# A two-layer hybrid encoder trunk: where the statistics of the MLP norm stand among the block products

## The chip, the cores and the metric

The kernel runs on one core of a Trainium2 chip. Its time is device microseconds of one execution; the figure quoted is the median of several. Times inside an execution come from one profiled execution, in microseconds from the start of its span. Engines: PE (TensorE), DVE (VectorE), ACT (ScalarE), POOL (GpSimd) and SP, which issues most of the DMAs.

## The reference, cut to what matters

```python
for i in range(DEPTH):                      # DEPTH = 2; D_MODEL = SEQ = 1024, D_FF = 4096
    h = rmsnorm(x, norm_mix_g[i])
    ...                                     # layer 0: RWKV-7 and DeltaNet heads; layer 1: chunked attention
    x = x + mix
    hf = rmsnorm(x, norm_ffn_g[i])
    x = x + jnp.square(jax.nn.relu(hf @ mlp_w1[i])) @ mlp_w2[i]
    x = x + rmsnorm(p[i] @ ple_w_proj[i], ple_norm_g[i]) * jax.nn.sigmoid(x @ ple_w_gate[i])

def rmsnorm(x, g, eps=NORM_EPS):
    xf = x.astype(jnp.float32)
    y = xf * lax.rsqrt(jnp.mean(xf * xf, -1, keepdims=True) + eps)
    return (y * g.astype(jnp.float32)).astype(x.dtype)
```

The norm in question is the one before the MLP. Its row factor is one number for each of the 1024 positions. Since relu(c z)^2 = c^2 relu(z)^2 for a positive c, the kernel multiplies by the square of that factor behind the first MLP product, not ahead of it, so the first products can run before the factor is known.

## The kernel before, in words

The program has a mixer stage and a function `tail` for each of the two layers. Activations are held transposed, features in the 128 partitions and the 1024 positions along the free dimension, in two halves of 512. Every float32 product is made of three matmuls of a high and a low part (`mm3`).

`tail` first finishes the output projection of the mixer and writes the new x to DRAM (`self.xh`, `self.xh2`, eight row blocks each). The MLP follows in a block scheme with seven products where eight are usual. The first MLP product is cut into 16 units `p`. In a unit there are seven block products (`product(p, m)`, 12 matmuls of 128x512 each, so 84 in a unit) in the order m = 1, 2, 5, 6, 7, 3, 4; slot (p, q) is the q-th of them. Their left operands are split weights, prepared one unit ahead by `prepare` (on ACT and DVE); their right operands `cmb[m]` stand in tiles that the profile calls `r` (m = 1, 2, 7, 3), `xw` and `x` (m = 5, 6) and `act` (m = 4). The results are combined on DVE (`plus`, L1375), then squared by `hidden` on ACT (L1380, L1381). The first four units (`PLAIN`) store the result without the row factor. From unit 4 on `hidden` multiplies by `rs` (L1385), so `rs` must be ready there.

`rs` is made in three steps:

- `squares(n)`, for n = 0 to 7: two DMAs on SP's queue bring the two halves of block n into one tile `xq` (L1315), ACT squares each half in place (L1317), and DVE adds it to one of two accumulators `acc` (L1318). There is one buffer for `xq`, so a DMA waits for the two adds of the block before.
- `row_stats`: eight matmuls against a column of ones (the profile's `dps<-ones,acc`, two instructions each, four matmuls for each accumulator), and on DVE eleven small operations of 128x8, of which the last nine are three Newton steps for the inverse root in `col` (L289, L290, L291).
- `to_rows`: eight transposes of `col` (`dps<-ident,col`), two copies by ACT into `rs` (L386), and one squaring on DVE (L1496).

The instructions are written out in program order, and a scheduler with a timeline of its own then sets the order in each engine's queue. Each queue is worked off in that order. The results of all products go to a ring of eight PSUM banks (`bank`), which the statistics use too.

Of the kernel before, what the change touches and what calls it, by code (L numbers as in the profile page):

```python
# [12 lines left out]
ALU = mybir.AluOpType  # L13
# [7 lines left out]
NK = D // P  # L21
# [88 lines left out]
class Trunk:  # L110
# [1092 lines left out]
    def tail(self, i, xsrc):  # L1203
# [10 lines left out]
        V, A, G = nc.vector, nc.scalar, nc.gpsimd  # L1214
        last = i == 1
        hs = [slice(0, HB), slice(HB, T)]
        with ExitStack() as es:
# [28 lines left out]
            def tiles_x(dt):  # L1246
                xw = [self.xp.tile([P, 3, T], dt, tag=f"xw{q}", name=f"xw{q}") for q in range(2)]
                return ([xw[k // 3][:, k % 3, :] for k in range(6)] +
                        [self.xp.tile([P, T], dt, tag=f"x{k}", name=f"x{k}") for k in (6, 7)])
# [11 lines left out]
            accs = [self.accp.tile([P, HB], F32, tag=f"acc{hf}", name="acc") for hf in range(2)]  # L1261
            col = self.cst.tile([P, NT], F32, tag="col", name="col")
# [4 lines left out]
            def split(c, s):  # L1267

                hi, lo = c[:, 0], c[:, 1]
                if len(s.shape) > 2:  # L1270
                    hi, lo = (z.rearrange("p (j c) -> p j c", c=P) for z in (hi, lo))
                A.copy(hi, s)  # L1272
                V.tensor_tensor(lo, s, hi.bitcast(F32), op=ALU.subtract)  # L1273
# [36 lines left out]
            def squares(n):  # L1310

                both = self.pre.tile([P, 2, HB], F32, tag="pl", name="xq")
                for hf, src in ((0, self.xh[n]), (1, self.xh2[n])):
                    t = both[:, hf]
                    nc.sync.dma_start(out=t, in_=src)  # L1315
                    if n:
                        A.activation(t, t, AF.Square)  # L1317
                        V.tensor_tensor(accs[hf], accs[hf], t, op=ALU.add)  # L1318
                    else:
                        A.activation(accs[hf], t, AF.Square)  # L1320
# [3 lines left out]
            def raws(p):  # L1324
                r = lt[3 - p % 2] if p else place(F32)
                for e in range(2):
                    nc.sync.dma_start(out=r[:, e], in_=a["w1"][i, 2 * p + e])
                prep[p] = [r[:, u].rearrange("p (j e c) -> p e j c", e=2, c=P)[:, v] for u in range(2) for v in range(2)], {}, []

            def prepare(p, m):  # L1330

                (a11, a12, a21, a22), d, free = prep[p]
                if (p, m) == (0, 1):
                    d[m] = self.pre.tile([P, 2, HB], F32R, tag="pl", name="w1")
                else:
                    if not free:
                        free += parts(place(F32R))
                    d[m] = free.pop(0)
                if m == 5:

                    V.tensor_tensor(a21, a21, a22, op=ALU.add)
                o, u, v = {1: (a11, None, None), 2: (a12, None, None), 5: (a21, None, None), 6: (a11, a21, a11),
                           4: (a22, None, None), 7: (a22, a22, a11), 3: (a12, a12, a11)}[m]
                if u is not None:
                    V.tensor_tensor(o, u, v, op=ALU.subtract)
                split(d[m], o)
# [16 lines left out]
            rs = self.pre.tile([P, T], F32, tag="ph", name="rs")  # L1363


            def product(p, m):
                ps, c = self.bank(), prep[p][1][m]
                for j in range(4):
                    o, z = slice(j * P, j * P + P), cmb[m][j]
                    self.mm3(ps, c[:, 0, o], c[:, 1, o], z[:, 0], z[:, 1], j == 0, j == 3)  # L1370
                return ps

            def plus(t, u, out=None):
                r = out if out is not None else scr()
                V.tensor_tensor(r, t, u, op=ALU.add)  # L1375
                return r

            def hidden(t, p, r, hf):

                A.activation(t, t, AF.Relu)  # L1380
                A.activation(t, t, AF.Square)  # L1381
                if p < PLAIN:
                    nc.scalar.dma_start(out=self.hd[2 * p + r][:, hs[hf]], in_=t)
                else:
                    V.tensor_tensor(t, t, rs[:, hs[hf]], op=ALU.mult)  # L1385
                    if (r, hf) != (0, 1):
                        store(p, {(0, 0): 1, (1, 0): 2, (1, 1): 3}[r, hf], t)
                return t
# [4 lines left out]
            def differ(p, m, u, v, out=None):  # L1393
                t = out if out is not None else scr()
                V.tensor_tensor(t, u, v, op=ALU.subtract)
                store(p, m, t)
                return t
# [4 lines left out]
            def load_w2(g, u):  # L1402
                t, raw = place(F32R), self.pre.tile([P, 2, HB], F32, tag="pl", name="w2")
                for j in range(2):
                    nc.sync.dma_start(out=raw[:, j], in_=a["w2"][i, 2 * g + j, u])
                split(t, raw.rearrange("p j c -> p (j c)"))
                w2[g, u] = t[:, 0], t[:, 1]

            def fetch_hidden(g, k, t, raw):
                nc.sync.dma_start(out=raw, in_=self.hd[4 * g + k])  # L1410
                return t, raw

            def load_hidden(t, raw):
                V.tensor_tensor(raw, raw, rs, op=ALU.mult)
                split(t, raw)
# [32 lines left out]
                split(areas[m][q % 4], raw)  # L1448

            prep_order = (1, 2, 5, 6, 4, 7, 3)  # L1450
            for m in prep_order[1:]:
                prepare(0, m)
            for p in range(16):
                if p < 15:
                    raws(p + 1)
                else:
                    load_w2(0, 0)
                for q, m in enumerate(order):
                    ps = product(p, m)
                    if m == 1:  # L1460
                        p1 = scr()
                        A.copy(p1, ps)
                    elif m == 2:
                        c11 = hidden(plus(p1, ps), p, 0, 0)
                    elif m == 5:
                        p5 = ps
                    elif m == 6:
                        u2 = plus(p1, ps, p1)
                        u4 = plus(u2, p5)
                    elif m == 7:  # L1470
                        u3 = plus(u2, ps, u2)
                        c22 = hidden(plus(u3, p5), p, 1, 1)
                    elif m == 3:
                        c12 = hidden(plus(u4, ps, u4), p, 0, 1)
                        if p >= PLAIN:
                            differ(p, 7, c22, c12)
                            t1 = differ(p, 5, c12, c11, c12)
                            t2 = differ(p, 6, c22, t1)
                    else:
                        c21 = hidden(plus(u3, ps, u3), p, 1, 0)  # L1480
                        if p >= PLAIN:
                            differ(p, 4, c21, t2)
                    if p < 15:
                        prepare(p + 1, prep_order[q])
                    elif q == 1:
                        hid = [fetch_hidden(0, k, h0[k], lt[2 + k // 2][:, k % 2]) for k in range(4)]
                    elif 2 <= q < 6:
                        load_hidden(*hid[q - 2])
                    yield 0
                if p < 3:  # L1490
                    for n in range(3 * p, min(3 * p + 3, NK)):
                        squares(n)
                if p == 2:
                    self.row_stats(accs, col)
                    self.to_rows(col, rs)
                    V.tensor_tensor(rs, rs, rs, op=ALU.mult)  # L1496
            x = tiles_x(F32)
            for k in range(NK):
                nc.sync.dma_start(out=x[k][:, hs[0]], in_=self.xh[k])
# [602 lines left out]
```

## Time and profile before

| | |
|---|---|
| median of 3 runs | 3133.64 us (3126.05 to 3135.7) |
| the profiled execution | 3130.04 us, its span 3128.3 us |
| mean granted TensorE clock | 0.968 |
| PE busy | 3000.5 us, 96% of the span |
| DVE busy | 2234.1 us, 71% |
| ACT busy | 1510.6 us, 48% |
| squares, first and last DMA, layer 0 | 999.88 and 1045.47 us |
| statistics on PE, layer 0 | 1050.03 to 1059.4 us |
| squares, first and last DMA, layer 1 | 2406.13 and 2451.93 us |
| statistics on PE, layer 1 | 2456.86 to 2463.4 us |

A busy PE is not a PE at its peak: the granted clock is 1.0 or 0.5, and matmuls overlap. In a timeline, each row has the start, the time until the last of the group has ended, the engine, the line, the operation with its tiles, the count and, in brackets, the idle time ahead of it and what ended that.

### The profile page before, as it was taken

What the parts mean: (1) busy time and instruction counts of PE and PEld (TensorE: products, weight loads), DVE (VectorE), ACT (ScalarE), POOL (GpSimd) and SP (SyncE); (2) the same over time, 40 slices, a digit from 0 to 9 for tenths busy, and PEclk for the clock granted to TensorE, in tenths of its full rate; (3) what the DMA queues carried; (4) which work ended last, traced back from release to release, by engine and by line L of the source; (5) the groups of instructions that cost most, each with busy time, mean ns of one, the idle gap of its engine ahead of it and who ended that gap; (6) DMA issues with size and microseconds to landing.
All of it is one profiled execution on the core that took longest, in us unless ns stands there. A gap on an engine that the chain in (4) does not pass through costs nothing.

```text
span 3128.3 us, 47113 instructions
## 1 busy us (share of the span) xinstructions
PE 3000.5 (96%) x17288; PEld 2476.6 (79%) x17288; DVE 2234.1 (71%) x4518; ACT 1510.6 (48%) x2922; POOL 532.5 (17%) x978
## 2 busy tenths in 40 slices
PE   7999999999999999999999898999899999999999
PEld 5777777777777788888888888988888788888887
DVE  6646675667758688888866576777768788888862
ACT  4323442434426544444433577777766544444431
POOL 6524443434510000000005210111110000000002
PEclk8989999999999999999999999999999999999999
DMA  3212112212346444754433211110156444654433
GB/s 130 77 43 69 47 44 79 63 56 64 105 159 205 151 152 148 247 177 151 130 108 118 68 36 33 46 35 19 67 181 205 152 155 148 239 182 149 135 107 103
DMA packets 187639, 358.45 MB, mean 115 GB/s; under 512 B 45712, under 2 KB 47888, under 8 KB 187408
## 3 DMA queue, kind: packets, MB, share of 16 engines
q1 hardware_dynamic: 158608, 303.00, 29.9%
q10 hardware_dynamic: 28800, 52.44, 4.4%
q8 instruction: 136, 2.23, 0.3%
q14 instruction: 95, 0.78, 0.1%
HBM read 262.04 MB, written 93.32 MB: 114 GB/s over the span
## 4 chain that ended last, share of the span: by engine, by line
PE 79%; DVE 10%; ACT 4%; DMA 3%; issue 2%; POOL 1%; SPq 0%; DVEq 0%; ACTq 0%; POOLq 0%
PE dps L177 67%; PE ch L177 2%; PE pm L177 1%; PE po L177 1%; PE tp L177 1%; PE iz L177 1%; DVE ptile L350 1%; PE pt L192 1%; DVE f L1058 1%; PE sn L177 1%; PE py L177 1%; DVE pb L1942 1%; ACT pb L1955 1%; DVE wlo L304 1%; POOL subt L415 1%
## 5 line engine op out<-in xcount | busy, mean ns | idle before, releaser
L177 PE MATMUL dps<-r,act 128*128 128x512 f32 x3528 | 831.5, 393 | 0.0
L177 PEld LDWEIGHTS dps<-r,act 128*128 128x128 f32 x3528 | 665.0, 189 | 146.7
L177 PE MATMUL dps<-xg,whi 128*128 128x512 f32 x1280 | 439.1, 424 | 16.6 <-ACT xg L352 7.4
L1599 POOL TENSOR_TENSOR pn<-pn,prs 128x512 f32<-128x512 f32 x32 | 45.5, 1424 | 1578.2 <-ACT prs L386 1481.8
L177 PE MATMUL dps<-wq,act 128*128 128x384 f32 x1536 | 306.3, 345 | 7.7 <-DVE vs L1851 3.7
L177 PEld LDWEIGHTS dps<-xg,whi 128*128 128x128 f32 x1280 | 238.1, 198 | 67.8 <-ACT xg L352 7.4
L177 PEld LDWEIGHTS dps<-wq,act 128*128 128x128 f32 x1536 | 267.2, 192 | 12.1 <-DVE vs L1851 6.1
L177 PE MATMUL dps<-xg,wlo 128*128 128x512 f32 x640 | 261.5, 410 | 1.9 <-DVE wlo L304 1.9
L177 PE MATMUL dps<-late,act 128*128 128x512 f32 x960 | 229.3, 392 | 0.0
L177 PEld LDWEIGHTS dps<-late,act 128*128 128x128 f32 x960 | 180.3, 188 | 39.7
L1272 ACT CAST act<-act 128x512 fp32r<-128x512 f32 (+1 forms) x223 | 137.7, 648 | 129.5 <-PE dps L177 67.4
L1375 DVE TENSOR_TENSOR late<-late,dps 128x512 f32<-128x512 f32 x224 | 152.3, 684 | 62.1 <-PE dps L177 53.7
L1272 ACT CAST act<-late 128x512 fp32r<-128x512 f32 x210 | 124.3, 618 | 136.2 <-PE dps L177 89.3
L177 PE MATMUL dps<-act 128*128 128x512 f32 x672 | 165.2, 392 | 0.0
L1273 DVE TENSOR_TENSOR act<-act 128x512 fp32r<-128x512 f32 (+1 forms) x223 | 155.0, 722 | 5.9 <-ACT act L1272 5.7
L303 ACT CAST whi<-wraw 128x1024 fp32r<-128x1024 f32 x78 | 81.6, 1047 | 154.1 <-PE dps L177 90.3
L177 PEld LDWEIGHTS dps<-xg,wlo 128*128 128x128 f32 x640 | 125.9, 197 | 33.2 <-DVE wlo L304 4.1
L1273 DVE TENSOR_TENSOR act<-late,act 128x512 fp32r<-128x512 f32 x210 | 141.3, 687 | 11.2 <-ACT act L1272 9.3
L177 PEld LDWEIGHTS dps<-act 128*128 128x128 f32 x672 | 126.2, 188 | 28.7
L1507 DVE TENSOR_TENSOR xw<-xw,dps 128x512 f32<-128x512 f32 x174 | 118.0, 683 | 32.4 <-PE dps L177 32.2
L177 PE MATMUL dps<-xw,act 128*128 128x512 f32 x576 | 138.5, 391 | 0.0
L1380 ACT ACTIVATE late<-late 128x512 f32<-128x512 f32 x128 | 80.2, 629 | 118.4 <-DVE late L1375 112.0
(484 smaller groups left out, 5656.2 us busy)
## 6 DMA issues: line engine op xcount, KB each, us to landing
hb<-late ACTq DMA_DIRECT2D x168, 256.0 KB
act<-hb SPq DMA_DIRECT2D x138, 256.0 KB
late<-in_w SPq DMA_DIRECT2D x60, 512.0 KB
wraw<-in_w_in SPq DMA_DIRECT2D x56, 512.0 KB
act<-in_w SPq DMA_DIRECT2D x96, 256.0 KB
braw<-hb SPq DMA_DIRECT2D x72, 256.0 KB
wraw<-in_w_out SPq DMA_DIRECT2D x21, 512.0 KB
wraw<-in_w_qkv SPq DMA_DIRECT2D x21, 512.0 KB
```

The lines of the kernel that those rows point to most:

```text
L177: return self.begin(self.nc.tensor.matmul(out, lhsT, rhs, start=start, stop=stop, skip_group_check=again))
L192: return self.begin(self.nc.tensor.transpose(out, in_, ident))
L303: nc.scalar.copy(hi, raw)
L304: nc.vector.tensor_tensor(lo, raw, hi.bitcast(F32), op=ALU.subtract)
L350: nc.vector.tensor_tensor(dst[:, 1, sl], src, dst[:, 0, sl].bitcast(F32), op=ALU.subtract)
L415: E.tensor_tensor(o, X[:, 0:i, i:i + 1].broadcast_to((NP, i, n)), Bq[:, i:i + 1, i + 1:16].broadcast_to((NP, i, n)), op=ALU.mult)
L1272: A.copy(hi, s)
L1273: V.tensor_tensor(lo, s, hi.bitcast(F32), op=ALU.subtract)
L1375: V.tensor_tensor(r, t, u, op=ALU.add)
L1380: A.activation(t, t, AF.Relu)
L1507: V.tensor_tensor(x[n][:, hs[hf]], x[n][:, hs[hf]], ps, op=ALU.add)
L1599: G.tensor_tensor(pn, pn, prs[:, sl], op=ALU.mult)
```

## The change

In program order `squares` moves from the ends of units 0, 1 and 2 (three, three and two calls) into eight single slots of the units 0 to 2. `row_stats` moves from the end of unit 2 to slot (3, 0), and `to_rows` with the squaring of `rs` to slot (3, 3). No operation is added or removed.

```diff
             prep_order = (1, 2, 5, 6, 4, 7, 3)
+            sums = [(0, 1), (0, 3), (0, 6), (1, 1), (1, 4), (1, 6), (2, 2), (2, 4)]
...
                     elif 2 <= q < 6:
                         load_hidden(*hid[q - 2])
+                    if (p, q) in sums:
+                        squares(sums.index((p, q)))
+                    elif (p, q) == (3, 0):
+                        self.row_stats(accs, col)
+                    elif (p, q) == (3, 3):
+                        self.to_rows(col, rs)
+                        V.tensor_tensor(rs, rs, rs, op=ALU.mult)
                     yield 0
-                if p < 3:
-                    for n in range(3 * p, min(3 * p + 3, NK)):
-                        squares(n)
-                if p == 2:
-                    self.row_stats(accs, col)
-                    self.to_rows(col, rs)
-                    V.tensor_tensor(rs, rs, rs, op=ALU.mult)
```

What the scheduler makes of it can be seen in the queues. On SP the DMAs of both tails, those of the squares among them, stand in the same places as before. On ACT and DVE the squares stand within a few rows of where they stood. What moves is the statistics.

PE in layer 0, from the last product of unit 2 to the first products of unit 3; `dps_11021` and `dps_11038` are unit 3's m = 5 and 6, `dps_10985` its m = 1. Before:

```order
L177 MATMUL dps_10913<-act_10137,act_10734 128x512 x6
L177 MATMUL dps_11021<-xw0_10132,act_10850 128x512 x9
L177 MATMUL dps_11021<-xw1_10133,act_10850 128x512 x3
L177 MATMUL dps_11038<-xw1_10133,act_10850 128x512 x6
L177 MATMUL dps_11038<-x6_10134,act_10850 128x512 x3
L177 MATMUL dps_11038<-x7_10135,act_10850 128x512 x3
L177 MATMUL dps_10948<-ones_67,acc_10143 128x1 x4
L177 MATMUL dps_10948<-ones_67,acc_10144 128x1 x4
L192 MATMUL dps_10970<-ident_62,col_10145 128x128 x4
L192 MATMUL dps_10976<-ident_62,col_10145 128x128 x4
L177 MATMUL dps_10985<-r_10121,act_10815 128x512 x6
```

The same place now, where `dps_10950` and `dps_10989` are unit 3's m = 1 and 2, `dps_11008` its m = 5:

```order
L177 MATMUL dps_10927<-act_10137,act_10741 128x512 x6
L177 MATMUL dps_10950<-r_10121,act_10815 128x512 x6
L177 MATMUL dps_10950<-r_10122,act_10815 128x512 x6
L177 MATMUL dps_10967<-ones_67,acc_10143 128x1 x4
L177 MATMUL dps_10989<-r_10123,act_10815 128x512 x6
L177 MATMUL dps_10989<-r_10124,act_10815 128x512 x6
L177 MATMUL dps_11008<-xw0_10132,act_10850 128x512
L177 MATMUL dps_10967<-ones_67,acc_10144 128x1 x4
L177 MATMUL dps_11008<-xw0_10132,act_10850 128x512 x8
```

The first four products with the ones stand behind 12 matmuls of unit 3 where they stood behind 24, the other four 13 matmuls later. The transposes (not shown) stand 37 matmuls behind these, in unit 3's m = 3.

PE in layer 1, from the last product of unit 2 (`dps_23867` before, `dps_23881` now). Before:

```order
L177 MATMUL dps_23867<-act_23088,act_23688 128x512 x6
L177 MATMUL dps_23902<-ones_67,acc_23094 128x1 x4
L177 MATMUL dps_23902<-ones_67,acc_23095 128x1 x4
L192 MATMUL dps_23924<-ident_62,col_23096 128x128 x4
L192 MATMUL dps_23930<-ident_62,col_23096 128x128 x4
L177 MATMUL dps_23939<-r_23066,act_23769 128x512 x6
```

Now, where `dps_23904`, `dps_23943` and `dps_23962` are unit 3's m = 1, 2 and 5:

```order
L177 MATMUL dps_23881<-act_23088,act_23695 128x512 x6
L177 MATMUL dps_23904<-r_23066,act_23769 128x512 x6
L177 MATMUL dps_23904<-r_23067,act_23769 128x512 x6
L177 MATMUL dps_23943<-r_23068,act_23769 128x512 x6
L177 MATMUL dps_23943<-r_23069,act_23769 128x512 x6
L177 MATMUL dps_23962<-xw0_23083,act_23804 128x512 x3
L177 MATMUL dps_23921<-ones_67,acc_23094 128x1 x4
L177 MATMUL dps_23921<-ones_67,acc_23095 128x1 x4
L177 MATMUL dps_23962<-xw0_23083,act_23804 128x512 x6
```

All products with the ones stand behind 27 matmuls of unit 3 where they stood behind none. The transposes (not shown) stand 33 matmuls further on, behind the first product of unit 4.

The scheduler also orders the attention of layer 1 anew, which the change does not touch in the program: on DVE the queue differs from about 1839 us of the profile to the start of the second tail. PE there, in the first place that differs (`sn` and `sf` are scores, `po` the weighted sum, `pt` transposes):

```order
 L177 MATMUL sn<-F_16781,Ql 128x256
 L177 MATMUL po<-ptile,vs 128x128 x3
-L177 MATMUL sn<-F_16781,F_16794 128x384
-L177 MATMUL sn<-F_16781,Ql 128x384
 L177 MATMUL sf<-F_16781,F_16794 128x128
 L177 MATMUL sf<-F_16781,Ql 128x128
 L177 MATMUL sn<-F_16781,F_16794 128x384
 L177 MATMUL sn<-F_16781,Ql 128x384
+L177 MATMUL sn<-F_16781,F_16794 128x384
+L177 MATMUL sn<-F_16781,Ql 128x384
+L192 MATMUL pt<-ident,pb 128x128 x2
```

One pair of score products has moved behind two others. Many such places follow.

## The prediction

> **What bounds the kernel now.** I read the page first, then the granted clock and PE's timeline around the statistics, then what the statistics wait for.
>
> ```profile
> span 3128.3 us, 47113 instructions
> PE 3000.5 (96%) x17288; PEld 2476.6 (79%) x17288; DVE 2234.1 (71%) x4518; ACT 1510.6 (48%) x2922; POOL 532.5 (17%) x978
> 1100.00:1630.00 530.00, 530.00 (x2317) 434.19 (x2316) 431.15 (x665) 238.62 (x391) 3.01 (x2) 1.00 0.47 159
> 2490.00:3100.00 610.00, 610.00 (x2667) 499.78 (x2666) 468.50 (x716) 257.85 (x422) 16.53 (x13) 1.00 0.46 155
> ```
>
> The last two rows are stretches of the two tails: length, busy time of PE, PE's weight loads, DVE, ACT and POOL, then PE's clock, the DMA share and GB/s. PE has no idle time in either. So in the tails PE sets the end, and what PE gains at the statistics isn't given back behind them. PE in layer 0, then in layer 1:
>
> ```profile
> 1041.29 4.24 PE L177 MATMUL dps<-xw,act 128*128 128x512 f32 x18
> 1045.37 1.52 PE L177 MATMUL dps<-x,act 128*128 128x512 f32 x6
> 1050.03 3.57 PE L177 MATMUL dps<-ones,acc 128*128 128x1 f32 x16 [3.14 <-DVE acc L1318]
> 1057.45 1.97 PE L192 MATMUL dps<-ident,col 128*128 128x128 f32 x8 [3.85 <-DVE col L291]
> 1059.07 13.30 PE L177 MATMUL dps<-r,act 128*128 128x512 f32 x48
> ...
> 1074.96 5.67 PE L177 MATMUL dps<-r,act 128*128 128x512 f32 x24
> ...
> 1094.24 5.67 PE L177 MATMUL dps<-r,act 128*128 128x512 f32 x24
> ```
> ```profile
> 2451.59 2.93 PE L177 MATMUL dps<-act 128*128 128x512 f32 x12
> 2456.86 1.05 PE L177 MATMUL dps<-ones,acc 128*128 128x1 f32 x8 [2.35 <-DVE acc L1318]
> 2458.07 1.05 PE L177 MATMUL dps<-ones,acc 128*128 128x1 f32 x8 [0.15 <-DVE acc L1318]
> 2461.39 1.97 PE L192 MATMUL dps<-ident,col 128*128 128x128 f32 x8 [2.27 <-DVE col L291]
> 2463.01 7.33 PE L177 MATMUL dps<-r,act 128*128 128x512 f32 x24
> ...
> 2483.94 5.67 PE L177 MATMUL dps<-r,act 128*128 128x512 f32 x24
> ```
>
> An undisturbed unit of 84 matmuls takes 1094.24 - 1074.96 = 19.28 us, 0.2295 us a matmul. Unit 3 takes 1074.96 - 1041.29 = 33.67 us in layer 0. In layer 1 unit 2 ends one step behind its last matmul's start, at 2451.59 + 12 x 0.2295 = 2454.35, and unit 3 with the statistics takes 29.59 us. So the statistics cost 14.39 and 10.31 us: idle time, their own products, and products at half clock behind them:
>
> ```profile
> 1048.00:1050.00 2.00, 0.00 (x0) 0.00 (x0) 0.99 (x3) 1.17 (x2) 0.00 (x0) 0.97 0.38 145
> 1050.00:1052.00 2.00, 1.97 (x10) 1.97 (x10) 1.87 (x3) 0.71 (x2) 0.00 (x0) 0.50 0.00 0
> 1064.00:1066.00 2.00, 2.00 (x10) 1.67 (x9) 0.00 (x0) 0.59 (x1) 0.00 (x0) 1.00 0.00 0
> 2458.00:2460.00 2.00, 1.05 (x8) 0.97 (x8) 1.86 (x8) 1.31 (x3) 0.00 (x0) 0.89 0.40 123
> 2466.00:2468.00 2.00, 2.00 (x9) 1.60 (x9) 0.00 (x0) 0.38 (x1) 0.00 (x0) 0.90 0.00 0
> ```
>
> The clock falls to 0.50 near 1049.9, some 3 us behind the last block product (1045.37 + 6 x 0.2295 puts its end at 1046.75), and is back by 1064. In layer 1 it falls near 2459.6 and is back near 2466. The 24 matmuls behind the wait in layer 1 take 7.33 - 5.67 = 1.66 us longer than 24 at full clock.
>
> **The change part by part.** Nothing is added or removed. The squares' 32 DMAs (two for each of eight blocks, two layers) keep their places on SP, and their ACT and DVE operations nearly so; I cost them at nothing, since PE runs through units 0 to 2 without a gap behind either order. What remains is what PE finds when it meets the statistics. In layer 0 the last block of squares sets that:
>
> ```profile
> 1044.39 0.68 DVE L1318 TENSOR_TENSOR acc<-acc,xq 128x512 f32<-128x512 f32 x1
> 1045.10 0.32 SPq L1315 DMA_DIRECT2D xq<-xh  x1
> 1048.62 0.63 ACT L1317 ACTIVATE xq<-xq 128x512 f32<-128x512 f32 x1 [1.07 <-DMA xq<-xh]
> 1049.28 0.69 DVE L1318 TENSOR_TENSOR acc<-acc,xq 128x512 f32<-128x512 f32 x1 [1.01 <-ACT xq L1317]
> ...
> 1056.63 0.69 DVE L1341 TENSOR_TENSOR late<-late 128x512 f32<-128x512 f32 x1 [1.01 <-DMA late<-in_w]
> 1057.24 0.16 DVE L291 SCALAR_TENSOR_TENSOR col<-rsw,col 128x8 f32<-128x8 f32 x1
> ```
>
> The DMA of block 7 starts 0.03 us behind block 6's last add (the one buffer), takes 3.5 us, and the first accumulator is done at 1049.97. Nothing new stands ahead of this chain in its queues, but for one copy of unit 3's m = 1 (ACT, about as long as the other ACT operations, 0.6 us), which falls into ACT's 1.07 us of idle time; without that cover it would cost its 0.6 us. So PE can start the statistics at 1050.03, as before. It comes there with 12 matmuls of unit 3 done, at 1041.29 + 2.75 = 1044.04, and waits 5.99 us: the stall ahead of the ones grows from 3.14 us, since it now has 12 matmuls of cover, not 24. Queued behind the waiting product are all of unit 3's other matmuls, and the engines that evacuate them.
>
> From 1050.03 on, layer 0: the first four products with the ones at half clock, half of 3.57, 1.8 us; the other 72 matmuls 72 x 0.2295 = 16.52; the other four with the ones 1.05 (the row of layer 1 at full clock); the transposes at full clock, from this row two groups of 0.55 to 0.60, 1.1 us;
>
> ```profile
> 1802.12 0.60 PE L192 MATMUL dps<-ident,qk 128*128 128x128 f32 x4
> 1060.00:1090.00 30.00, 30.00 (x125) 24.39 (x124) 17.18 (x26) 12.10 (x21) 0.00 (x0) 0.94 0.32 101
> ```
>
> and half clock behind the wait, 1.66 as in layer 1. That ends unit 3 at 1072.2, against 1074.96: **2.8 us saved**. The wait of 3.85 us for `col` is gone: 37 matmuls, 8.5 us, stand between the ones and the transposes, and eleven small operations are done 3.6 us after the ones when nothing is in between (1053.64 to 1057.24), where before the last of them also stood behind a weight sum that waited 1.01 us for its DMA. The ACT copies and the squaring of `rs` now lie inside unit 3, where DVE is busy 17.18 of 30 us; unit 4 is the first to need them, half a unit later. Bounds: if the clock stays up, 0.75 less for the ones and 1.66 less, 5.2 saved; if half clock lasts 6.8 us, as between 2459.6 and 2466.4, 3.4 lost of which 1.66 is counted, 1.1 saved.
>
> Layer 1: the accumulators are done when the ones start there, 2456.86 and 2458.07. PE now comes after 27 matmuls, at 2454.35 + 6.20 = 2460.55, 2.5 us behind the later one. So no wait, and 33 matmuls (7.6 us) cover `col`. Unit 3 costs 19.28 + 2.1 + 1.1 = 22.5, against 29.59: **7.1 us saved**. Lower bound: if the last squares slip by more than the 2.5 us, PE stalls as in layer 0 and 2.8 is left.
>
> [...]
>
> The attention of layer 1 gets another order:
>
> ```profile
> 1800.00:1860.00 60.00, 55.77 (x363) 52.25 (x362) 42.24 (x135) 46.24 (x108) 6.49 (x6) 1.00 0.12 39
> 1800.00:2220.00 420.00, 386.23 (x2465) 363.98 (x2464) 293.51 (x970) 307.86 (x733) 44.38 (x49) 0.98 0.10 34
> ```
>
> PE is idle for 33.8 of these 420 us, since it waits on chains through ACT and DVE. The operations are the same, so only this idle time can change, up or down. The first 60 us have 4.2 us of it, 12% below the mean of 4.8; taking a swing of that kind to a fifth, I put 7 us on either side and 0 in the middle.
>
> Sum: 2.8 + 7.1 = 9.9 us. The profiled execution's 3130.04 us (1.74 us outside its span) would become 3120.1; it lies 3.6 us below the median of the runs shown, so the forecast for the median is 3133.64 - 9.9 = **3123.7 us**, 0.32% faster.
>
> **The rivals.**
>
> 1. *The clock stays up in layer 0*, because the wait ends before it falls: it fell 3.1 us behind the last product before, which speaks against it. 2.4 more saved, 3121.3. Chance 0.10.
> 2. *The new attention order is the worse one*: a score or weighted sum whose softmax isn't ready stands at the head of PE's queue, and PE's idle 33.8 us there grow. From 9.9 us more (29%) it eats the gain; I price it at 40%, 13.5 us, which gives 3137.2. For it: an order that differs over some 350 us; against it: same operations, same dependencies. Chance 0.12.
> 3. *The attention gains over 7 us*: 3115. As likely by the same rows: 0.13.
> 4. *The statistics don't really come earlier*: the queues show the squares where they were, and if in layer 1 the last block slips as well, only 2 x 2.8 are left, 3128.0. Against it: 2.5 us of margin. Chance 0.07.
>
> **How the numbers follow.** The forecast has 0.58: 3123.7, from 3118 to 3130 with the bounds of layer 0 and half the swing of the attention. The range 3112 to 3136 leaves out the far halves of rivals 2 and 3 and a little of the scatter of single medians (before, 3126.05 to 3135.7). Faster or slower by over 0.3% is 9.4 us, about what a measurement of this kernel can tell from no change: the limits are 3124.2 and 3143.0. Just over half of the forecast's chance (0.33), most of rival 1 (0.08) and rival 3 (0.13) are below the first: 0.54. Half of rival 2, with a far tail of the attention, is above the second: 0.09. The rest, 0.37, is within.
>
> **What would show it.** Right: in layer 0 a single wait of about 6 us ahead of the first ones, for `acc`, none ahead of the transposes, and unit 3 at 30.9 us; in layer 1 no wait at either place, clock 1.0 throughout, and unit 3 at 22.5 (25.3 with the first product of unit 4, which now lies inside it). Wrong: a wait for `acc` in layer 1, a wait at the transposes, a gap behind unit 3, or a change of PE's idle time between 1800 and 2220 us by more than 7 us.

## The result, and the profile after

| | before | after |
|---|---|---|
| median | 3132.02 us (3126.05 to 3136.78, 8 runs) | 3120.34 us (3112.93 to 3128.76, 8 runs) |
| the profiled execution | 3130.04 us | 3117.76 us |
| its span | 3128.3 us | 3116.0 us |

The ratio is 0.9967, with a 95% interval of 0.9955 to 0.998: about 10.3 us faster, with the interval from 6.3 to 14.1 us. The two medians are 11.7 us apart, which lies inside it. The forecast was 3123.7 us and 0.32%.

The profile page of after, its span and the busy time of the engines (share of the span, instructions):

```profile
span 3116.0 us, 47110 instructions
...
PE 2994.4 (96%) x17288; PEld 2471.7 (79%) x17288; DVE 2229.9 (72%) x4518; ACT 1511.9 (49%) x2922; POOL 536.3 (17%) x978
```

PE's timeline of after, first unit 3 of layer 0, then the same place in layer 1 (start, time until the last of the group has ended, count, and in brackets the idle time ahead and its releaser):

```profile
1042.77 2.93 PE L177 MATMUL dps<-act 128*128 128x512 f32 x12
1045.54 2.93 PE L177 MATMUL dps<-r,act 128*128 128x512 f32 x12
1053.64 1.87 PE L177 MATMUL dps<-ones,acc 128*128 128x1 f32 x8 [5.17 <-DVE acc L1318]
1055.38 5.44 PE L177 MATMUL dps<-r,act 128*128 128x512 f32 x12
1060.64 0.41 PE L177 MATMUL dps<-xw,act 128*128 128x512 f32 x1
1060.89 0.95 PE L177 MATMUL dps<-ones,acc 128*128 128x1 f32 x8
1061.70 4.14 PE L177 MATMUL dps<-xw,act 128*128 128x512 f32 x17
...
1070.26 1.04 PE L192 MATMUL dps<-ident,col 128*128 128x128 f32 x8
1071.05 2.55 PE L177 MATMUL dps<-r,act 128*128 128x512 f32 x10
...
1076.18 5.67 PE L177 MATMUL dps<-r,act 128*128 128x512 f32 x24
...
2446.93 2.93 PE L177 MATMUL dps<-act 128*128 128x512 f32 x12
2449.70 5.67 PE L177 MATMUL dps<-r,act 128*128 128x512 f32 x24
2455.21 0.86 PE L177 MATMUL dps<-xw,act 128*128 128x512 f32 x3
2455.91 1.84 PE L177 MATMUL dps<-ones,acc 128*128 128x1 f32 x16
2457.61 3.69 PE L177 MATMUL dps<-xw,act 128*128 128x512 f32 x15
...
2465.26 1.04 PE L192 MATMUL dps<-ident,col 128*128 128x128 f32 x8
2466.06 5.74 PE L177 MATMUL dps<-r,act 128*128 128x512 f32 x24
2471.63 2.93 PE L177 MATMUL dps<-act 128*128 128x512 f32 x12
```

In layer 0 one wait is left, ahead of the products with the ones; the one at the transposes is gone, and unit 3 takes 1076.18 - 1045.54 = 30.64 us (33.67 before). In layer 1 both waits are gone. There unit 3 begins at 2446.93 + 12 x 0.2295 = 2449.68 and ends at 2471.63 + 12 x 0.2295 = 2474.38; without the 12 matmuls of unit 4 that now lie inside it takes 21.94 us (29.59 before).

The granted clock (the number behind the busy times) shows where it was halved. Stretches of after, around the wait of layer 0 and the statistics of layer 1:

```profile
1050.00:1052.00 2.00, 0.00 (x0) 0.00 (x0) 0.00 (x0) 0.00 (x0) 0.00 (x0) 0.60 0.82 231
1058.00:1060.00 2.00, 2.00 (x6) 1.53 (x5) 0.00 (x0) 0.00 (x0) 0.00 (x0) 0.50 0.00 0
1060.00:1062.00 2.00, 2.00 (x12) 1.73 (x12) 1.15 (x2) 1.04 (x2) 0.00 (x0) 0.83 0.00 0
2454.00:2460.00 6.00, 6.00 (x35) 5.19 (x35) 4.91 (x15) 3.25 (x6) 0.00 (x0) 1.00 0.54 176
```

A mean of 0.60 over the 2 us from 1050.00 puts the fall to 0.50 at 1050.4, and 0.83 over the 2 us from 1060.00 puts the return at 1060.7. In layer 1 the clock stays at 1.00 (mean from 2446 to 2475).

### The profile page after: what moved, and what is told of

The parts are those of the page before. It is cut to its first block, busy times and chain, and to the rows that moved or that the text cites. A ratio compares the mean times of both kernels' runs of the same rounds, so it can differ in the third digit from the quotient of the medians.

```text
span 3116.0 us, 47110 instructions
## 1 busy us (share of the span) xinstructions
PE 2994.4 (96%) x17288; PEld 2471.7 (79%) x17288; DVE 2229.9 (72%) x4518; ACT 1511.9 (49%) x2922; POOL 536.3 (17%) x978
## 4 chain that ended last, share of the span: by engine, by line
PE 78%; DVE 10%; ACT 5%; DMA 3%; issue 2%; POOL 2%; SPq 0%; DVEq 0%; POOLq 0%; ACTq 0%
PE dps L177 66%; PE ch L177 2%; PE po L177 1%; PE pm L177 1%; PE tp L177 1%; PE iz L177 1%; PE pt L192 1%; DVE f L1058 1%; DVE ptile L350 1%; DMA wraw<-in_w_out 1%; ACT pb L1956 1%; PE sn L177 1%; POOL subt L415 1%; DMA wraw<-in_w_qkv 1%; DVE wlo L304 1%
```

## The experiments

All ratios are against the kernel before, in runs beside it; the medians of different rows come from different groups of runs, so the ratios are what to compare. Stage times come from each kernel's profile; unit 3 is measured as above.

| kernel | ratio | median, us | unit 3, layer 0 | unit 3, layer 1 |
|---|---|---|---|---|
| before | 1 | 3132.02 | 33.67 | 29.59 |
| after | 0.9967 (0.9955 to 0.998) | 3120.34 | 30.64 | 21.94 |
| layer 0 only | 0.9986 (0.9972 to 1.0) | 3124.55 | 30.90 | 31.13 |
| layer 1 only | 0.9972 (0.996 to 0.9984) | 3120.93 | 33.12 | 21.95 |
| statistics only | 0.995 (0.9936 to 0.9965) | 3116.0 | 30.78 | 21.94 |
| squares only | 0.9998 (0.9986 to 1.0011) | 3130.27 | 33.81 | 31.39 |
| statistics at slots (3, 2) and (3, 5) | 0.9933 (0.9911 to 0.9954) | 3108.23 | 21.95 | 22.00 |
| statistics at slots (3, 4) and (3, 6) | 0.9935 (0.9916 to 0.9955) | 3109.29 | 21.85 | 21.9 |
| after, two buffers for `xq` | 0.9943 (0.9925 to 0.9961) | 3110.89 | 21.93 | 21.92 |
| slots (3, 2) and (3, 5), two buffers | 0.9937 (0.9919 to 0.9955) | 3110.14 | 22.00 | 22.0 |
| before, two buffers | 0.9955 (0.9939 to 0.997) | 3117.73 | 21.90 | 28.79 |

### One layer at a time

In layer 0 only (for layer 1 only, 1 stands for 0):

```diff
-                    if (p, q) in sums:
+                    if i == 0 and (p, q) in sums:
                         squares(sums.index((p, q)))
-                    elif (p, q) == (3, 0):
+                    elif i == 0 and (p, q) == (3, 0):
                         self.row_stats(accs, col)
-                    elif (p, q) == (3, 3):
+                    elif i == 0 and (p, q) == (3, 3):
...
+                if i != 0 and p < 3:
+                    for n in range(3 * p, min(3 * p + 3, NK)):
+                        squares(n)
+                if i != 0 and p == 2:
+                    self.row_stats(accs, col)
...
```

> The change in layer 0's tail alone; layer 1's tail as before. On the queues the attention of layer 1 gets the new order too. Theory (the statistics' waits alone): unit 3 of layer 0 takes 30.6 us for 33.7, so 3 us faster, ratio 0.999. Rival (the new attention order carries part of the gain): 3 us plus the 6 us that lay between the two tails in the changed kernel's profile, 9 us faster, ratio 0.997.

> The change in layer 1's tail alone; layer 0's tail and the attention keep the order of before. Theory: unit 3 of layer 1 takes 22 us for 29.6, so 7.6 us faster, ratio 0.9976. Rival (the attention carries the gain, the tails little): under 4 us, ratio above 0.9987.

Each layer does its own part, in the place that the change touches: 30.90 us in layer 0 with layer 1 as it was (31.13), and 21.95 us in layer 1 with layer 0 as it was (33.12). The ratios are 0.9986 and 0.9972, so about 4.4 and 8.8 us. They agree with stage savings of some 3 and 8 us, but the first interval ends at 1.0: layer 0 alone can't be told from no change by the total, only by the stage. In the queues, the kernel with the change in layer 0 only has the new order of the attention, and that with layer 1 only has the old one. So the 8.8 us of the second came without the new order, and 0.997, which the rival gave for the first, lies just outside its interval.

### Statistics alone, squares alone

Statistics only (edit of after):

```diff
-                    if (p, q) in sums:
-                        squares(sums.index((p, q)))
-                    elif (p, q) == (3, 0):
+                    if (p, q) == (3, 0):
                         self.row_stats(accs, col)
...
                     yield 0
+                if p < 3:
+                    for n in range(3 * p, min(3 * p + 3, NK)):
+                        squares(n)
```

Squares only (edit of after):

```diff
                     if (p, q) in sums:
                         squares(sums.index((p, q)))
-                    elif (p, q) == (3, 0):
-                        self.row_stats(accs, col)
-                    elif (p, q) == (3, 3):
-                        self.to_rows(col, rs)
-                        V.tensor_tensor(rs, rs, rs, op=ALU.mult)
                     yield 0
+                if p == 2:
+                    self.row_stats(accs, col)
+                    self.to_rows(col, rs)
+                    V.tensor_tensor(rs, rs, rs, op=ALU.mult)
```

> The squares at the ends of units 0, 1 and 2 as before, the statistics in slots (3, 0) and (3, 3) as in the change. Its queues are those of the change row for row. Theory: as the change, 10 us faster, ratio 0.9967. Rival (the single slots of the squares do it): half of it or less, ratio above 0.998. The profile is a second look at the changed queues: segments that differ between two looks at the same queues are scatter.

> The squares in their single slots as in the change, the statistics at the end of unit 2 as before. Its queues are those of before row for row. Theory: ratio 1.000, unit 3 of layer 0 at 33.7 us and of layer 1 at 29.6 us. Rival (the single slots do it): ratio 0.998 or less. The profile is a second look at the queues of before.

The change is two edits, and only one acts. With the squares alone the engines' queues are row for row those of before, and the ratio is 0.9998. With the statistics alone they are row for row those of after. The slot in which the squares are written decides nothing here; that the scheduler goes by when their data is ready would explain it, but was not tested. Squares only, PE in layer 0 and then in layer 1:

```profile
1054.32 3.57 PE L177 MATMUL dps<-ones,acc 128*128 128x1 f32 x16 [3.25 <-DVE acc L1318]
1062.00 1.97 PE L192 MATMUL dps<-ident,col 128*128 128x128 f32 x8 [4.11 <-DVE col L291]
...
2459.66 3.07 PE L177 MATMUL dps<-ones,acc 128*128 128x1 f32 x16 [3.06 <-DVE acc L1318]
...
2466.61 7.60 PE L177 MATMUL dps<-r,act 128*128 128x512 f32 x24
```

All the waits of before are there. Statistics only, PE in layer 0:

```profile
1050.62 2.93 PE L177 MATMUL dps<-r,act 128*128 128x512 f32 x12
1058.81 1.87 PE L177 MATMUL dps<-ones,acc 128*128 128x1 f32 x8 [5.26 <-DVE acc L1318]
...
1081.40 5.67 PE L177 MATMUL dps<-r,act 128*128 128x512 f32 x24
```

This is the picture of after, 5 us later: 12 matmuls, the wait, unit 3 at 30.78 us. Its total came out lower than that of after (0.995 and 0.9967, intervals that overlap from 0.9955 to 0.9965) with the same queues, so 1.7 per mille between two kernels here tells nothing of their edits.

### What the wait of layer 0 is made of

The squares' chain of after: the last add of block 6, the DMA of block 7, its squaring, its first add.

```profile
1048.61 0.69 DVE L1318 TENSOR_TENSOR acc<-acc,xq 128x512 f32<-128x512 f32 x1
1049.32 0.32 SPq L1315 DMA_DIRECT2D xq<-xh  x1
1052.24 0.63 ACT L1317 ACTIVATE xq<-xq 128x512 f32<-128x512 f32 x1 [2.52 <-DMA xq<-xh]
1052.90 0.69 DVE L1318 TENSOR_TENSOR acc<-acc,xq 128x512 f32<-128x512 f32 x1 [3.01 <-ACT xq L1317]
```

Block 7's DMA starts 0.02 us behind block 6's last add, since both use the one buffer, and 3.8 us behind the start of unit 3. Two theories of how to be rid of the wait: more products ahead of the statistics, or an earlier DMA. The first moves the statistics two slots on (the second kernel of this kind to (3, 4) and (3, 6)):

```diff
-                    elif (p, q) == (3, 0):
+                    elif (p, q) == (3, 2):
                         self.row_stats(accs, col)
-                    elif (p, q) == (3, 3):
+                    elif (p, q) == (3, 5):
                         self.to_rows(col, rs)
```

> As the change, but the statistics two slots later: products with the ones in slot (3, 2), transposes in (3, 5). On PE's queue the ones of layer 0 stand behind 53 matmuls of unit 3 (12.2 us) for 12. Theory (PE waits in layer 0 because the last accumulator is done 8.1 us behind unit 2's end and only 2.75 us of matmuls cover it): no wait ahead of the ones, clock 1.0, unit 3 of layer 0 at 22 us, so 8 us faster than the change and 18 us faster than before, ratio 0.994; a short wait at the transposes is possible, 19 matmuls (4.4 us) behind the ones. Rival (the wait is for something that moves along, or the later row factor stalls unit 4): no faster than the change, 0.9967.

> As the change, but the statistics four slots later: ones in slot (3, 4), transposes in (3, 6). On PE's queue the ones stand behind 60 matmuls, the transposes of layer 0 behind 32 more, ahead of unit 4's first product. Theory: no wait at either place, ratio 0.994 as with two slots later; the first multiplications by the row factor in unit 4 come close, and if they stall, a gap in unit 4 of 1 to 3 us. Rival: no faster than the change, 0.9967.

PE of the kernel with slots (3, 2) and (3, 5), layer 0:

```profile
1042.39 5.67 PE L177 MATMUL dps<-r,act 128*128 128x512 f32 x24
...
1054.58 1.84 PE L177 MATMUL dps<-ones,acc 128*128 128x1 f32 x16
...
1060.73 1.03 PE L192 MATMUL dps<-ident,col 128*128 128x128 f32 x8
...
1064.34 5.67 PE L177 MATMUL dps<-r,act 128*128 128x512 f32 x24
```

Now 53 matmuls, 1054.58 - 1042.39 = 12.19 us, stand ahead of the ones, and there is no wait and no half clock (the granted clock is 1.00 from 1042 to 1066). Unit 3 takes 21.95 us, 8.7 less than after. Two slots later still there is nothing more to have (21.85), and the gap in unit 4 that I thought possible isn't there.

The second theory gives `xq` another buffer, by letting every other block use the place of `rs`, which is then made just ahead of its first use:

```diff
-                both = self.pre.tile([P, 2, HB], F32, tag="pl", name="xq")
+                both = self.pre.tile([P, 2, HB], F32, tag="p" + "lh"[n % 2], name="xq")
...
-            rs = self.pre.tile([P, T], F32, tag="ph", name="rs")
...
                     elif (p, q) == (3, 3):
+                        rs = self.pre.tile([P, T], F32, tag="ph", name="rs")
                         self.to_rows(col, rs)
```

> As the change, but the squares take turns in two buffers (the second is the space of the row factor, which is allocated after them). Theory (the one buffer makes each DMA wait for the adds of the block before, so the last add comes 8.1 us behind unit 2's end): block 7's DMA no longer waits for block 6's adds and starts at least 4 us earlier, the wait of 5.4 us ahead of the ones in layer 0 shrinks below 2 us, and the clock stays at 1.0: 5 to 8 us faster than the change, ratio 0.9945. Rival (the DMAs are late for another reason, the queue of SP or the transfer): the wait stays above 4 us and the time with the change's, 0.9967.

> Both: statistics two slots later and two buffers for the squares. Theory: nothing is left to wait for once either is done, so as two slots later alone, ratio 0.994. Rival (each removes a different wait): 5 us faster than either.

Two buffers: the DMA of block 7 and the last add, then PE in layer 0.

```profile
1024.70 0.32 SPq L1315 DMA_DIRECT2D xq<-xh  x1
...
1032.40 0.69 DVE L1318 TENSOR_TENSOR acc<-acc,xq 128x512 f32<-128x512 f32 x1
...
1041.03 2.93 PE L177 MATMUL dps<-r,act 128*128 128x512 f32 x12
1043.80 1.84 PE L177 MATMUL dps<-ones,acc 128*128 128x1 f32 x16
1045.50 3.01 PE L177 MATMUL dps<-r,act 128*128 128x512 f32 x12
...
1053.83 1.04 PE L192 MATMUL dps<-ident,col 128*128 128x128 f32 x8
1054.62 5.75 PE L177 MATMUL dps<-r,act 128*128 128x512 f32 x24
...
1062.96 1.32 PE L177 MATMUL dps<-r,act 128*128 128x512 f32 x5
```

The accumulators are done at 1033.09, 8 us ahead of unit 3, so 12 matmuls ahead of the ones are plenty. Unit 3 takes 1062.96 - 1041.03 = 21.93 us, the same as with more cover (products that PE works on meanwhile). Both edits together give no more (22.00): they remove the same wait.

### Two buffers, statistics at the old place

The same two edits on before, with `rs` made behind `row_stats` at the end of unit 2.

> Two buffers for the squares, and the statistics at the end of unit 2 as before (the change undone but for the second buffer). On PE's queue the ones of both layers stand straight behind unit 2; in layer 0 the transposes stand behind 24 matmuls of unit 3, in layer 1 straight behind the ones. Theory (two waits: the accumulators, which the one buffer delays, and the chain of eleven small operations for the inverse root, which needs cover): no wait for the accumulators in either layer, unit 3 of layer 0 at 22 us, in layer 1 a wait of 2.3 to 2.7 us for the root with unit 3 at 24.5 us, or up to 28 if the clock falls; 16 us faster than before, ratio 0.995. Rival (the place of the statistics is what matters, the buffer only in company with it): waits for the accumulators stay above 2 us and the ratio above 0.998.

In layer 0 it did as well as the others: unit 3 takes 21.90 us, since the scheduler puts 24 matmuls between the ones and the transposes. Layer 1 is a miss for the theory: the wait for `acc` is gone, but the one for `col` is 5.37 us, where I had put down 2.3 to 2.7. PE, and then DVE, in layer 1:

```profile
2441.16 2.93 PE L177 MATMUL dps<-act 128*128 128x512 f32 x12
2443.93 1.84 PE L177 MATMUL dps<-ones,acc 128*128 128x1 f32 x16
2451.14 1.97 PE L192 MATMUL dps<-ident,col 128*128 128x128 f32 x8 [5.37 <-DVE col L291]
2452.76 6.37 PE L177 MATMUL dps<-r,act 128*128 128x512 f32 x24
```
```profile
2446.63 0.69 DVE L1341 TENSOR_TENSOR late<-late 128x512 f32<-128x512 f32 x1 [0.32 <-DMA late<-in_w]
2447.23 0.69 DVE L1273 TENSOR_TENSOR act<-late,act 128x512 fp32r<-128x512 f32 x1
2447.84 0.69 DVE L1345 TENSOR_TENSOR late<-late 128x512 f32<-128x512 f32 x1
2448.44 0.16 DVE L375 TENSOR_SCALAR ms<-dps 128x8 f32<-128x8 f32 x1
...
2450.91 0.17 DVE L291 SCALAR_TENSOR_TENSOR col<-rsw,col 128x8 f32<-128x8 f32 x1
```

The products with the ones are done at about 2445.6, but the first of the eleven small operations starts only at 2448.44: full-size preparations of weights stand ahead of it in DVE's queue, the first of them behind a wait for its own DMA. The small ones, with one full-size operation among them, then take 2450.91 + 0.17 - 2448.44 = 2.64 us. The clock is at 0.50 from 2447.1 to 2453.9, and unit 3 takes 28.79 us. So the root needs cover on PE as well as the accumulators; a second buffer supplies the one and not the other.

## Why the prediction was right, step by step

**PE sets the end in the tails.** Right. The stretches of the two tails behind unit 3 (unit 4 of layer 0 to the first product of layer 1's first weights, and the rest behind unit 3 of layer 1) took 638.42 and 644.36 us before, and 638.43 and 644.36 after: nothing that was gained at the statistics was given back.

**The squares cost nothing.** Right, and shown more sharply than I had it: the squares alone change no queue, and the ratio is 0.9998.

**Layer 0, 2.8 us saved, unit 3 at 30.9.** Right: 30.64, and over three profiles with the old place (33.67, 33.81, 33.12) and three with the new (30.64, 30.78, 30.90) the means are 33.53 and 30.77, 2.8 apart. That the sum fits to 0.3 us is partly luck: inside, four terms were off and nearly cancelled. The wait was 1053.64 - (1045.54 + 2.75) = 5.35 us, not 5.99, as the DMA took 2.9 us until ACT began, not 3.5. The half clock behind it cost more: 12 matmuls took 5.26 us, from 1055.38 to 1060.64, so 2.5 us too long and not 1.66. The second four ones and the transposes took 0.81 and 0.79 us, not 1.05 and 1.1. The 3.6 us put down for the eleven small operations "when nothing is in between" held the wait of a weight sum; in layer 1 of before they take 2.2 us, from 2459.16 to 2461.34. Nothing in the sum hangs on it. Rival 1, the clock that stays up, fell.

**Layer 1, 7.1 us saved, no wait.** The mechanism was right, the size too small: 7.65 us between the two profiles, and 8.8 over three and three (29.59, 31.39, 31.13 with the old place; 21.94, 21.94, 21.95 with the new). The term that was mis-sized most is what the old place costs: its profile before had 6.8 us of half clock, the other two 10.2. The statistics' own products, put at 3.2 us, cost 1.70 + 0.80 = 2.5. Rival 4 fell.

**The attention at 0, with 7 us on either side.** PE's busy time where the prediction looked is unchanged, 386.23 and 386.20 us. But those 420 us of after hold 18 matmuls more, so the time of the whole stage says more. After, from 1800 to 2220 us:

```profile
1800.00:2220.00 420.00, 386.20 (x2483) 363.65 (x2482) 297.59 (x983) 311.10 (x738) 46.69 (x49) 0.98 0.10 34
```

The stage from the first product of layer 1's weights to its unit 3 took 740.97, 738.71 and 737.26 us in the three profiles with the old order, and 735.09, 736.12, 738.25, 737.71 and 738.42 in the five with the new (after, statistics only, layer 0 only, the two with later slots). The means are 739.0 and 737.1; the scatter within a group is as large. Between before and after it is 5.9 us, but that goes with less half clock: added up over short stretches, 30.6 us from 1745 to 2350 before and 20.4 after. So rivals 2 and 3 aren't borne out, and whether the new order is worth a microsecond or two stays open.

**The sum.** 9.9 us were forecast; the stages give 2.8 + 8.8 = 11.6, the ratio 10.3. The interval of the ratio is 4 us wide on either side, and layer 1 was put 1.7 us too low, so it is luck that 9.9 and 10.3 lie so close. The places of the gain, the waits of the two tails, were forecast rightly.

In layer 0 of after the clock fell at 1050.4, 2.1 us behind the last block product (12 matmuls from 1045.54 end at 1048.29). In the row of before that the prediction held against rival 1 it fell 3.1 us behind it (1046.75 to 1049.9). So the time from the last product to the fall was not the same twice. That the clock would fall in this wait was forecast rightly; what sets the moment was not shown. When it returned at 1060.7, PE had worked without a gap for 7.0 us, from 1053.64 on, the first 1.7 us of them on products with the ones.

## What to carry to other kernels

A reduction that PE must make between block products needs cover twice: products ahead of it while its operands are finished, and products between it and the use of what the other engines make of it. PE waited 5.35 us in layer 0 of after, where the first fell short, and 5.37 in layer 1 of before with two buffers, where the second was missing. With both, little more is left than its own PE time: unit 3 takes 21.9 to 22.0 us where a unit without statistics takes 19.28, and 2.5 of those 2.7 us are the statistics' own products. The same 8.7 us in layer 0 could be had by moving the statistics or by a second buffer, and not twice. Where a scheduler sets the order, compare the queues before believing that moved source lines do anything.

## What the runs showed of the hardware

**The same queues, 15 us apart.** Unit 3 of layer 0 began between 1035.8 and 1050.6 us in these profiles, and at 1041.29 and 1045.47 in the two kernels with before's queues, 1045.54 and 1050.62 in the two with after's. The earliest and the latest are slots (3, 4) and (3, 6) and statistics only, whose queues are the same up to unit 3. The first 1000 us of statistics only, and then of slots (3, 4) and (3, 6):

```profile
0.00:1000.00 1000.00, 946.15 (x7272) 732.74 (x7273) 638.14 (x1394) 391.36 (x785) 386.64 (x850) 0.92 0.27 86
```
```profile
0.00:1000.00 1000.00, 938.83 (x7337) 727.82 (x7338) 652.54 (x1415) 400.14 (x800) 383.17 (x850) 0.95 0.27 87
```

In those 1000 us the clock was at half for about 160 and 109 us, added up over short stretches, and 65 matmuls more were done in the second. Half clock isn't all of it: before had 136 us and began unit 3 at 1041.29, squares only had 126 and began it at 1045.47, and PE sat idle for 63.6 us ahead of it, against 55.7. A single pair of profiles says little about an edit worth 10 us in its total; the stage that the edit touches says it within some tenths where there is no half clock (layer 1, new place: 21.94, 21.94 and 21.95), and within two microseconds where there is (old place: 29.59, 31.39 and 31.13).

**When the clock falls and returns.** But for the first and the last of a trace, every stretch at one clock in the traces of before and after lasts a multiple of 3.41 us: half clock around the statistics of layer 0 lasted 13.65 us before and 10.24 after. In layer 0 only it lasted 6.83 there. In after the last 3.41 us ahead of the fall at 1050.4 held 1.3 us of block products (38%). In layer 0 only, the 3.41 us from 1041.73 to 1045.14 held about as much (39%), the clock was still at 1.00 behind them, and it fell at 1048.55, 5.5 us behind the last block product (12 matmuls from 1040.31 end at 1043.06). On the way back in after, half clock lasted 10.24 us after a wait of 5.35: from 1053.8 to 1057.2 PE made products with the ones and 1.9 us of block products, and the clock stayed at 0.50 until 1060.7. In before, the clock fell in layer 1 at 2459.6, 0.4 us behind the eight products with the ones (sixteen instructions), which PE had made from 2456.86 on. These are readings of a few falls against modelled ends of matmuls; what makes the clock fall or return they don't show.
